# GLA levels by growing queries and keys in place, and projection sections in another order

## The chip, the cores and the metric

One core of a Trainium2 chip runs one program. The metric is the device time of one execution in microseconds, as the median of several. The engines are TensorE (PE; its weight loads are listed as PEld), VectorE (DVE), ScalarE (ACT), GpSimd (POOL) and SyncE (SP), each with its own queue that runs in order, beside 16 DMA engines.

## The reference

One decoder layer over 512 tokens of width 1024, in float32: a token mixer of gated linear attention (GLA, 4 heads of key width 128 and value width 256) beside latent attention (8 heads), gated and projected, then a squared-ReLU MLP of width 4096, each with a residual and a layer norm. The part that the change touches is GLA:

```python
q_g, k_g, v_g, r_g, a_lr, q_lat, kv_lat, gate_logits = jnp.split(h @ w_in, offsets, axis=-1)
log_a = jax.nn.log_sigmoid(a_lr @ w_gla_a2 + b_gla_a2) / 16
# S_t = diag(a_t) S_{t-1} + k_t^T v_t,  o_t = q_t S_t
...
y_gla = (rms_norm(o_gla) * jax.nn.silu(r_g)) @ w_o_gla
```

In other words o_i is the sum over j <= i of (q_i . k_j, channel by channel times the product of the decays a over j+1..i) times v_j.

## The kernel before

Everything is kept transposed or by token tiles of 128. A float32 product is made of three matmuls on parts that are rounded to a shorter format: high by high, high by low, low by high. So each weight tile is loaded by SP (`wraw`), its high half is made by ACT (`whi`, line 180) and its low half by DVE (`wlo`, line 181). `pump` keeps the loads two and the splits one group ahead, in the order in which `plan` was called.

**Projection sections.** After the latents, queries and keys, the columns of `w_in` are multiplied in sections of 512 columns: 8 steps of 12 large matmuls each, into four PSUM banks. `proj_v(hp)` makes the values of heads 2hp and 2hp+1 and empties each bank by ACT (`vh`, line 106) and DVE (`vl`, line 107). `proj_r(hp)` makes the output gate: `th` is a tanh on ACT (line 600), `rg` a product on DVE that reads the bank (line 603). The gate sections `g` need one tanh on ACT for each bank (`gt`, line 958), and `mla_qr` makes the rotary queries. A section can start on a bank only when the one before has emptied it. The order is v0, r0, v1, r1, g0, g1, qr0, g2, g3, qr1 (g0 and g1 are the halves of the first branch's gate, g2 and g3 of the second's).

**Lanes.** Beside the sections run two generators, stepped once in each of a section's 8 steps: `lane_levels`, which makes the score matrices of the four heads in turn (`gla_levels`), and `lane_out`, which makes a head's output (`gla_out`) as soon as its scores, values and output gate are there. The order of the instructions in the queues is set by a scheduler when the program is built.

**Levels.** For each block size s = 1, 2, 4, ... 256 a level makes the scores between the right half of a block of 2s tokens (queries) and its left half (keys). `rp` holds two planes of 512 sums of log decays, for the keys from a token to the end of its block, for the queries from the start of the block. A level takes E = exp(rp/16) on ACT (line 651), multiplies by the queries and keys on DVE into M (line 658, two halves of 256 tokens; line 654 above 64), and doubles the reach of the sums on DVE (`advance`, line 634). PE multiplies M by itself (line 692; 695 at 128; transposes at 256, line 699), and DVE copies the result under a mask into `SD` (line 667). `products` makes the diagonal: `pr` on POOL (line 614), `qkp` high on ACT (616) and low on POOL (617), for the next head at s = 16.

Of the kernel before, what the change touches and what calls it, by code (L numbers as in the profile page):

```python
# [10 lines left out]
F32 = mybir.dt.float32  # L11
# [4 lines left out]
AF = mybir.ActivationFunctionType  # L16
# [3 lines left out]
P = 128  # L20
# [32 lines left out]
def tile_hybrid_block(ctx: ExitStack, tc: tile.TileContext, I, out, dbg=None):  # L53
# [50 lines left out]
    def split(src, hi, lo, scale=None):  # L104
        if scale is None:
            act(hi, src, AF.Copy)
# [31 lines left out]
    def plan(name, c0, n, k_lo=0, k_hi=None, heads=None, res=False, per=2):  # L138
        w = I[name]
        K = w.shape[0] // P  # L140
        k_hi = K if k_hi is None else k_hi
        idx = []
        for k0 in range(k_lo, k_hi, per):
            nk = min(per, k_hi - k0)
            if heads is None:
                src = w.rearrange("(k p) n -> p k n", p=P)
                dmas = [(slice(0, nk), src[:, k0:k0 + nk, c0:c0 + n], None)]
            else:
                hw, h0, nh = heads
# [135 lines left out]
        PL["lat", i] = plan("w_in", C_A + i * half, half, res=True)  # L285
    PL["q"] = plan("w_in", C_Q, T)
    PL["k"] = plan("w_in", C_K, T)
    for hp in range(2):
        PL["v", hp] = plan("w_in", C_V + hp * T, T)
        PL["r", hp] = plan("w_in", C_R + hp * T, T)  # L290
    def plan_qr(g):
        PL["qr", g] = plan("w_q_b", NOPE, 4 * ROPE, heads=(HQ, 4 * g, 4), per=4)

    for br in range(2):
        for mb in range(2):
            PL["g", br, mb] = plan("w_in", C_G + br * D + mb * T, T)
        plan_qr(br)

    def plan_pair(pr):
        PL["qn", pr] = plan("w_q_b", 0, 2 * P, heads=(HQ, 2 * pr, 2))  # L300
# [308 lines left out]

    QKP = [None] * GH  # L610

    def products(h, qk):
        pr = B([P, T], F32, "pr")
        gtt(pr, qk[:, 0, :], qk[:, 1, :], op=ALU.mult)
        QKP[h] = [B([P, T], F32R, "qkp") for _ in range(2)]
        act(QKP[h][0], pr, AF.Copy)
        gtt(QKP[h][1], pr, f(QKP[h][0]), op=ALU.subtract)

    def gla_levels(h):
        qk = QK[h]  # L620
        QK[h] = None
        rp = A([P, 2, T], F32, "rp")
        nc.vector.tensor_copy(rp[:, 1, :], GL[h])
        nc.gpsimd.memset(rp[:, 0, :], 0.0)
        SD = B([P, NT, P], F32, "SD")
        s128 = kq = None

        def advance(s):
            v = rp[:, 0, :]

            def view(off, side, step):
                return bass.AP(tensor=v.tensor, offset=v.offset + off, ap=[v.ap[0], [side, 2], [2 * s, T // (2 * s)], [step, s]])
            new = view(0, T + s, 1)
            vtt(new, new, view(T + 2 * s - 1, -s, 0), op=ALU.add)  # L634

        def half_lr(t2, s, i):
            v = t2[:, 0, :]
            return bass.AP(tensor=v.tensor, offset=v.offset + 2 * i * P,
                           ap=[v.ap[0], [2 * s, P // s], [T + s, 2], [1, s]])

        def packed(M, s, i):
            v = M[:, i, 0, :]
            return bass.AP(tensor=v.tensor, offset=v.offset,
                           ap=[v.ap[0], [2 * s, P // s], [s + (-2 * P if i else 2 * P), 2], [1, s]])

        def taken(v, s, step):
            return bass.AP(tensor=v.tensor, offset=v.offset + s, ap=[v.ap[0], [step, 2], [2 * s, P // s], [1, s]])

        def vec(s):
            E = B([P, T], F32, "E")  # L650
            act(pairs(E, s), lr(rp, s), AF.Exp, scale=1.0 / 16.0)  # L651
            if s > 64:
                M = B([P, T], F32, "M")
                vtt(pairs(M, s), pairs(E, s), lr(qk, s), op=ALU.mult)
            else:
                M = B([P, 2, 2, P], F32, "M")
                for i in range(2):
                    vtt(packed(M, s, i), pairs(E[:, 2 * i * P:2 * (i + 1) * P], s), half_lr(qk, s, i), op=ALU.mult)  # L658
            if s < 256:
                advance(s)  # L660
            return M

        def take(s, p):
            nonlocal s128, kq
            if s <= 64:
                mk = lmask[:, LEVELS.index(s)].rearrange("p o u (n s) -> p o (u n) s", s=s)
                nc.vector.copy_predicated(taken(SD[:, 0, :], s, 2 * P - s), mk, taken(p[:, :2 * P], s, -s))
            elif s == 128:
                s128 = B([P, 2, 2, P], F32R, "s128")
                split(p[:, :256].rearrange("p (a b) -> p a b", b=P), s128[:, 0], s128[:, 1])  # L670
            else:
                split(p[:, :256], kq[:, 0, 0], kq[:, 0, 1])


        if h == 0:
            products(0, qk)
        s = 1
        M = vec(1)
        yield
        diag = PX()  # L680
        for w in range(2):
            mm(diag, ones, QKP[h][w], start=w == 0, stop=w == 1)
        prev = None
        while s < T:
            if s == 2:
                vtt(SD, diag.rearrange("p (t i) -> p t i", i=P), ident[:, None, :].to_broadcast([P, NT, P]), op=ALU.mult)
            if s == 16 and h + 1 < GH:
                products(h + 1, QK[h + 1])
            p = PX()
            if s <= 64:  # L690
                for u in range(2):
                    mm(p[:, u * P:(u + 1) * P], M[:, 0, u, :], M[:, 1, u, :], start=True, stop=True)  # L692
            elif s == 128:
                for i in range(2):
                    mm(p[:, i * P:(i + 1) * P], M[:, 2 * i * P:(2 * i + 1) * P],
                       M[:, (2 * i + 1) * P:(2 * i + 2) * P], start=True, stop=True)
            else:
                for j in range(2):
                    nc.tensor.transpose(p[:, j * P:(j + 1) * P], M[:, j * P:(j + 1) * P], ident)
                kq = A([P, 2, 2, 256], F32R, "kq")  # L700
                split(M[:, 256:], kq[:, 1, 0], kq[:, 1, 1])
            if prev is not None:
                take(*prev)
            prev = (s, p)
            s *= 2
            if s < T:
                M = vec(s)
            yield
        sd = A([P, 2, NT, P], F32R, "sd")
        p = PX()  # L710
        for u in range(2):
            nc.tensor.transpose(p[:, u * P:(u + 1) * P], SD[:, 2 + u, :], ident)
        act(sd[:, 0, :2], SD[:, :2], AF.Copy)
        gtt(sd[:, 1, :2], SD[:, :2], f(sd[:, 0, :2]), op=ALU.subtract)
        take(*prev)
        yield
        pt = p[:, :2 * P].rearrange("p (u i) -> p u i", i=P)
        split(pt, sd[:, 0, 2:], sd[:, 1, 2:])
        SS[h] = (sd, s128, kq)
        if h != 2:  # L720
            yield
# [218 lines left out]
            step(t_lv)  # L940

    WID[0] = 3
    proj_v(0)
    proj_r(0)
    finish(t_lat2)
    proj_v(1)
    proj_r(1)
    t_gla = [t_lv, t_out]


    gt = [None] * NK
    for br in range(2):
        for mb in range(2):
            def ev_g(a, ps):
                m = mb * 4 + a
                if gt[m] is None:
                    gt[m] = A([P, 2, T], F32, "gt")
                act(gt[m][:, br, :], ps, AF.Tanh, scale=0.5, bias=hbg[:, br * NK + m:br * NK + m + 1])
            gemm_fm(PL["g", br, mb], hT, T, ev_g)
        mla_qr(br)  # L960
    hT = None


# [361 lines left out]
```

## Time and profile before

| | us |
|---|---|
| median of 3 runs | 888.38 |
| the three runs | 887.48, 892.6, 888.38 |
| the profiled execution, whole | 887.85 |
| its span, first to last instruction | 885.9 |
| PE busy, matmuls | 863.7 |
| DVE busy | 584.4 |
| ACT busy | 438.9 |
| POOL busy | 134.1 |

The profile is of one execution, 887.85 us long by the device's own count; the span that its tables cover is 2 us shorter. Matmuls overlap, so a matmul's duration is longer than its distance to the next one: the distance tells the rate. A row of a group shows the line, engine, operation, tiles (out<-in) and count, then busy us, mean ns of one, and the idle time of the engine just before them with who ended it. In a timeline a row is start, duration, engine, line, operation, and in brackets the idle time before it. The levels run from about 98 to 260 us of the span.

### The profile page before, as it was taken

Reading aid. Unit: us, or ns where it says so; the run is one execution under the profiler, and the core shown is the slowest. Engines: PE = TensorE matmul, PEld = TensorE weight load, DVE = VectorE, ACT = ScalarE, POOL = GpSimd, SP = SyncE. Lnnn points to the kernel's source line nnn. Section 1 sums busy time; section 2 is a strip of 40 time slices with the busy share of each in tenths; the row PEclk is TensorE's granted clock in tenths of the full one; section 3 lists DMA queues with packets and bytes.
Section 4 is the critical chain, followed back from the end, with each engine's and each line's share of the span. In section 5 each row is a group of like instructions: output and inputs, shape, how many; then the busy total and the mean of one; then the engine's idle time right before and its main releaser. Section 6 shows DMA issues by size and latency. Waiting matters only on the chain.

```text
span 885.9 us, 11470 instructions
## 1 busy us (share of the span) xinstructions
PE 863.7 (97%) x4336; PEld 735.9 (83%) x4336; DVE 584.4 (66%) x989; ACT 438.9 (50%) x737; POOL 134.1 (15%) x159
## 2 busy tenths in 40 slices
PE   5999999999999999999999999999999999999995
PEld 5988888887888888888888888988888888888884
DVE  7834894867665234557866797886557646754687
ACT  5546553634444334435654414565457546735661
POOL 2203320111002010000000013004400520242022
PEclk9999999999999999999999999999999999999998
DMA  7413223221323223111307628006941990398075
GB/s 235 145 48 95 72 72 95 72 72 48 90 72 88 74 84 101 54 43 54 116 25 264 190 71 285 1 0 164 293 114 29 260 253 28 71 305 195 1 189 96
DMA packets 63415, 101.13 MB, mean 114 GB/s; under 512 B 7777, under 2 KB 31764, under 8 KB 63360
## 3 DMA queue, kind: packets, MB, share of 16 engines
q1 hardware_dynamic: 48400, 64.04, 23.5%
q0 software_dynamic: 13040, 32.71, 15.5%
q10 hardware_dynamic: 1920, 3.66, 1.2%
q8 instruction: 34, 0.56, 0.3%
q14 instruction: 21, 0.17, 0.1%
HBM read 82.56 MB, written 3.67 MB: 97 GB/s over the span
## 4 chain that ended last, share of the span: by engine, by line
PE 95%; DVE 2%; ACT 1%; DMA 1%; issue 0%; POOL 0%; POOLq 0%; SPq 0%; DVEq 0%; ACTq 0%
PE mm L231 16%; PE mm L232 16%; PE mm L233 16%; PE mm L266 6%; PE mm L264 6%; PE mm L265 6%; PE px L1170 3%; PE px L1172 3%; PE px L1171 3%; PE mm L1170 2%; PE mm L1172 2%; PE mm L1171 2%; PE px L692 1%; PE px L868 1%; PE px L266 1%; PE px L265 1%
## 5 line engine op out<-in xcount | busy, mean ns | idle before, releaser
L181 DVE TENSOR_TENSOR wlo<-wraw,whi 128x1024 fp32r<-128x1024 f32 (+2 forms) x102 | 117.5, 1152 | 137.1 <-ACT whi L180 130.9
L231 PE MATMUL mm<-h,whi 128*128 128x512 f32 x416 | 163.3, 393 | 1.1 <-DVE rg L603 1.1
L232 PE MATMUL mm<-h,whi 128*128 128x512 f32 x416 | 163.0, 392 | 0.0
L233 PE MATMUL mm<-h,wlo 128*128 128x512 f32 x416 | 156.1, 392 | 0.0
L180 ACT ACTIVATE whi<-wraw 128x1024 fp32r<-128x1024 f32 (+2 forms) x102 | 99.9, 979 | 109.6 <-PE mm L232 66.3
L231 PEld LDWEIGHTS mm<-h,whi 128*128 128x128 f32 x416 | 78.6, 189 | 16.9 <-DVE rg L603 1.3
L232 PEld LDWEIGHTS mm<-h,whi 128*128 128x128 f32 x416 | 78.6, 189 | 16.0
L233 PEld LDWEIGHTS mm<-h,wlo 128*128 128x128 f32 x416 | 78.4, 189 | 16.1
L1198 POOL DMA_DIRECT2D res<-ev x54 | 47.5, 985 | 238.0 <-ACT ev L1196 190.7
L265 PE MATMUL mm<-wlo,h 128*128 128x512 f32 x128 | 50.5, 395 | 0.0
L266 PE MATMUL mm<-whi,h 128*128 128x512 f32 x128 | 50.3, 395 | 0.0
L264 PE MATMUL mm<-whi,h 128*128 128x512 f32 x128 | 49.2, 398 | 0.0
L1252 ACT ACTIVATE relu<-mm 128x512 f32<-128x512 f32 x32 | 18.8, 596 | 57.0 <-PE mm L233 57.0
L651 ACT ACTIVATE E<-rp 128x512 f32<-128x512 f32 x36 | 23.9, 665 | 28.3 <-DVE rp L634 27.4
L658 DVE TENSOR_TENSOR M<-E,qk 128x256 f32<-128x256 f32 x56 | 26.7, 501 | 15.4 <-ACT E L651 15.3
L355 POOL TENSOR_TENSOR mv<-mv,mhalf 128x1 f32<-128x1 f32 x4 | 4.1, 1036 | 208.9 <-DVE mv L354 208.9
L180 ACT ACTIVATE xh<-wraw 128x1024 fp32r<-128x1024 f32 (+1 forms) x20 | 19.0, 959 | 26.2 <-PE mm L266 15.0
L181 DVE TENSOR_TENSOR wlo<-wq,whi 128x1024 fp32r<-128x1024 f32 x15 | 18.4, 1224 | 20.3 <-ACT whi L180 20.3
L266 PEld LDWEIGHTS mm<-whi,h 128*128 128x128 f32 x128 | 24.1, 188 | 4.8
L265 PEld LDWEIGHTS mm<-wlo,h 128*128 128x128 f32 x128 | 24.1, 188 | 4.2
L264 PEld LDWEIGHTS mm<-whi,h 128*128 128x128 f32 x128 | 24.0, 188 | 4.1
L1196 ACT ACTIVATE ev<-mm 128x512 f32<-128x512 f32 x20 | 11.9, 600 | 29.6 <-DMA res<-ev 23.7
(400 smaller groups left out, 2223.6 us busy)
## 6 DMA issues: line engine op xcount, KB each, us to landing
wraw<-in_w_in_dram SPq DMA_DIRECT2D x40, 512.0 KB, 3.7
wraw<-in_w_ff_dram SPq DMA_DIRECT2D x32, 512.0 KB, 8.4
wq<-in_w_ff_dram POOLq DMA_DIRECT2D x32, 512.0 KB, 9.8
res<-ev POOLq DMA_DIRECT2D x54, 256.0 KB, 8.7
wraw<-in_w_o_gla_dram SPq DMA_DIRECT2D x8, 512.0 KB, 3.8
wraw<-in_w_o_mla_dram SPq DMA_DIRECT2D x8, 512.0 KB, 3.4
wraw<-in_w_out_dram SPq DMA_DIRECT2D x8, 512.0 KB, 4.3
wraw<-in_w_in_dram SPq DMA_DIRECT2D x8, 360.0 KB, 4.2
```

The source lines that it names most:

```text
L180: st["ins"] = act(hi[:, :nk, :n], raw[:, :nk, :n], AF.Copy)
L181: vtt(lo[:, :nk, :n], raw[:, :nk, :n], f(hi[:, :nk, :n]), op=ALU.subtract)
L231: mm(o, hi[:, c], xh, start=first, stop=False)
L232: mm(o, hi[:, c], xl, start=False, stop=False)
L233: mm(o, lo[:, c], xh, start=False, stop=last)
L264: mm(o, xh, hi[:, :n], start=opens, stop=False, skip_group_check=share)
L265: mm(o, xh, lo[:, :n], start=False, stop=False, skip_group_check=share)
L266: mm(o, xl, hi[:, :n], start=False, stop=last, skip_group_check=share)
L1170: mm(o, xh[:, c], hi[:, pp, cols], start=opens, stop=False, skip_group_check=True)
L1171: mm(o, xh[:, c], lo[:, pp, cols], start=False, stop=False, skip_group_check=True)
L1172: mm(o, xl[:, c], hi[:, pp, cols], start=False, stop=hf == 1 and pp == 1, skip_group_check=True)
L1198: nc.gpsimd.dma_start(res[tt + t][:, j * T:(j + 1) * T], e, accum_op=ALU.add)
```

## The change

Two things change.

First, the levels. Instead of sums of logarithms that are turned into factors anew in each level, the queries and keys themselves grow. `totals(h)` adds the gate logarithms of each block of 2, 4, ... 128 tokens on POOL (seven adds of 256 down to 4 elements), and takes exp of the gates and of all totals on ACT (two instructions). In `gla_levels` the queries are first multiplied by their own decay (DVE); after each level `grow` multiplies, in place, the right half's queries by the left half's total and the left half's keys by the right half's total (one DVE instruction of 128x512, as `advance` was). A level up to 64 then only packs q and k into M by two copies on ACT (`pack`); at 128 and 256 PE reads q and k themselves. `rp`, E, `advance` and the products M go. `totals(h + 1)` comes with `products(h + 1)` at s = 16.

Second, the order of the sections, in the plan of the weights and in the calls alike: r0, v0, g0, r1, v1, g2, qr0, g1, g3, qr1.

```diff
-    for hp in range(2):
-        PL["v", hp] = plan("w_in", C_V + hp * T, T)
-        PL["r", hp] = plan("w_in", C_R + hp * T, T)
+    ORDER = (("r", 0), ("v", 0), ("g", 0), ("r", 1), ("v", 1), ("g", 2), ("qr", 0), ("g", 1), ("g", 3), ("qr", 1))
...
+    TOT = [None] * GH
+
+    def totals(h):
+        t = TOT[h] = B([P, T], F32, "tot")
+        src, o, n = GL[h], 0, T // 2
+        while n >= 4:
+            a = src.rearrange("p (n two) -> p n two", two=2)
+            src = t[:, o:o + n]
+            gtt(src, a[:, :, 0], a[:, :, 1], op=ALU.add)
+            o += n
+            n //= 2
+        act(GL[h], GL[h], AF.Exp, scale=1.0 / 16.0)
+        act(t[:, :o], t[:, :o], AF.Exp, scale=1.0 / 16.0)
...
-        rp = A([P, 2, T], F32, "rp")
-        nc.vector.tensor_copy(rp[:, 1, :], GL[h])
-        nc.gpsimd.memset(rp[:, 0, :], 0.0)
...
-            new = view(0, T + s, 1)
-            vtt(new, new, view(T + 2 * s - 1, -s, 0), op=ALU.add)
+        def grow(s):
+            new = view(qk[:, 0, :], 0, T + s, 2 * s, 1, s)
+            tot, o = (GL[h], 0) if s == 1 else (TOT[h], T - 2 * T // s)
+            vtt(new, new, view(tot, o + 1, -1, 2, 0, s), op=ALU.mult)
...
-        def vec(s):
-            E = B([P, T], F32, "E")
-            act(pairs(E, s), lr(rp, s), AF.Exp, scale=1.0 / 16.0)
-            if s > 64:
-                M = B([P, T], F32, "M")
-                vtt(pairs(M, s), pairs(E, s), lr(qk, s), op=ALU.mult)
-            else:
-                M = B([P, 2, 2, P], F32, "M")
-                for i in range(2):
-                    vtt(packed(M, s, i), pairs(E[:, 2 * i * P:2 * (i + 1) * P], s), half_lr(qk, s, i), op=ALU.mult)
-            if s < 256:
-                advance(s)
+        def pack(s):
+            M = B([P, 2, 2, P], F32, "M")
+            for i in range(2):
+                act(packed(M, s, i), half_lr(qk, s, i), AF.Copy)
             return M
...
         if h == 0:
+            totals(0)
             products(0, qk)
+        vtt(qk[:, 1, :], qk[:, 1, :], GL[h], op=ALU.mult)
         s = 1
-        M = vec(1)
+        M = pack(1)
...
             if s == 16 and h + 1 < GH:
+                totals(h + 1)
                 products(h + 1, QK[h + 1])
...
-                    mm(p[:, i * P:(i + 1) * P], M[:, 2 * i * P:(2 * i + 1) * P],
-                       M[:, (2 * i + 1) * P:(2 * i + 2) * P], start=True, stop=True)
+                    mm(p[:, i * P:(i + 1) * P], qk[:, 0, 2 * i * P:(2 * i + 1) * P],
+                       qk[:, 1, (2 * i + 1) * P:(2 * i + 2) * P], start=True, stop=True)
...
             prev = (s, p)
+            if s < 256:
+                grow(s)
             s *= 2
-            if s < T:
-                M = vec(s)
+            if s <= 64:
+                M = pack(s)
...
-    proj_v(0)
-    proj_r(0)
-    finish(t_lat2)
-    proj_v(1)
-    proj_r(1)
...
+    for sec, i in ORDER:
+        if sec == "v":
+            proj_v(i)
+        elif sec == "r":
+            proj_r(i)
+            if i == 0:
+                finish(t_lat2)
+        elif sec == "g":
+            gates(i // 2, i % 2)
+        else:
+            mla_qr(i)
```

What it does to the queues is shown where the second output-gate section (r1) ends. PE there, before: the last two banks of r1 (`mm_1745`, `mm_1749`), the matmuls of levels 32 and 64 of the third head (`px_1954`, `px_1999`), and the first bank of g0 (`mm_2008`).

```order
L265 MATMUL mm_1745<-wlo_1870,h_33_171 128x512
L266 MATMUL mm_1745<-whi_1869,h_33_171 128x512
L264 MATMUL mm_1749<-whi_1869,h_33_171 128x512
L265 MATMUL mm_1749<-wlo_1870,h_33_171 128x512
L266 MATMUL mm_1749<-whi_1869,h_33_171 128x512
L692 MATMUL px_1954<-M_1924 128x128 x2
L692 MATMUL px_1999<-M_1960 128x128 x2
L231 MATMUL mm_2008<-h_12_115,whi_1938 128x512
```

PE there, in the changed kernel: the last bank of r1 (`mm_1727`), transposes of the second head's output (`og`), levels 32, 64 and 128 of the third head (`px_1927`, `px_1970`, `px_1991`), and the first bank of v1 (`mm_1975`).

```order
L264 MATMUL mm_1727<-whi_1836,h_33_171 128x512
L786 MATMUL px_1904<-ca,og_1828 128x128 x2
L786 MATMUL px_1904<-ca,og_1829 128x128 x2
L702 MATMUL px_1927<-M_1898 128x128 x2
L265 MATMUL mm_1727<-wlo_1837,h_33_171 128x512
L266 MATMUL mm_1727<-whi_1836,h_33_171 128x512
L702 MATMUL px_1970<-M_1932 128x128 x2
L705 MATMUL px_1991<-qk_750 128x128 x2
L264 MATMUL mm_1975<-whi_1911,h_12_115 128x512
```

Level 128 of that head now stands inside r1, behind level 64 with nothing between, and the section that follows is values, not a gate.

ACT at the same place, before: the last exp of the levels (`E`), the split of a weight tile, the head's output and the tanh of r1's first two banks (`mm_1737`, `mm_1741`).

```order
L651 ACTIVATE E_1889<-rp_1753 128x512
L180 ACTIVATE whi_1938<-wraw_1867 128x1024
L616 ACTIVATE qkp_1914<-pr_1912 128x512
L651 ACTIVATE E_1922<-rp_1753 128x512
L109 ACTIVATE ogT_1928<-px_1895,cb 128x512
L651 ACTIVATE E_1958<-rp_1753 128x512
L109 ACTIVATE ogT_1964<-px_1931,cb 128x512
L600 ACTIVATE th_1979<-mm_1737 128x512
L600 ACTIVATE th_1983<-mm_1741 128x512
```

ACT there, in the changed kernel: `M_1857`, `M_1898` and `M_1932` are the copies of levels 16, 32 and 64, `g_666` and `tot_1877` the next head's gates and totals.

```order
L667 ACTIVATE M_1857<-qk_750 128x8x2x16 x2
L180 ACTIVATE whi_1911<-wraw_1834 128x1024
L627 ACTIVATE g_666<-g_666 128x512
L634 ACTIVATE qkp_1889<-pr_1887 128x512
L109 ACTIVATE ogT_1901<-px_1860,cb 128x512
L667 ACTIVATE M_1898<-qk_750 128x4x2x32 x2
L628 ACTIVATE tot_1877<-tot_1877 128x508
L667 ACTIVATE M_1932<-qk_750 128x2x2x64 x2
L604 ACTIVATE th_1950<-mm_1715 128x512
```

The exp of the next head's totals stands ahead of level 64's copies and of the first tanh of r1.

POOL at the same place, before: the square-root scaling of a head (`grs`), the next head's diagonal, and a memset.

```order
L762 TENSOR_TENSOR grs_1837<-gss_1722,mhalf 128x4
L614 TENSOR_TENSOR pr_1912<-qk_752 128x512
L617 TENSOR_TENSOR qkp_1915<-pr_1912,qkp_1914 128x512
L624 MEMSET rp_2093 128x512
L714 TENSOR_TENSOR sd_2071<-SD_1756,sd_2071 128x256
```

POOL there, in the changed kernel:

```order
L774 TENSOR_TENSOR grs_1806<-gss_1700,mhalf 128x4
L624 TENSOR_TENSOR tot_1877<-g_666 128x256
L632 TENSOR_TENSOR pr_1887<-qk_752 128x512
L624 TENSOR_TENSOR tot_1877<-tot_1877 128x128
L624 TENSOR_TENSOR tot_1877<-tot_1877 128x64
L635 TENSOR_TENSOR qkp_1890<-pr_1887,qkp_1889 128x512
L624 TENSOR_TENSOR tot_1877<-tot_1877 128x32
L624 TENSOR_TENSOR tot_1877<-tot_1877 128x16
L624 TENSOR_TENSOR tot_1877<-tot_1877 128x8
L624 TENSOR_TENSOR tot_1877<-tot_1877 128x4
L726 TENSOR_TENSOR sd_2035<-SD_1731,sd_2035 128x256
```

Four of the seven adds stand behind the low half of `qkp`, which waits for ACT's high half.

More of the change, by code (lines that the diff above doesn't have):

```diff
@@ L287, in tile_hybrid_block @@
     PL["k"] = plan("w_in", C_K, T)
-    for hp in range(2):
-        PL["v", hp] = plan("w_in", C_V + hp * T, T)
-        PL["r", hp] = plan("w_in", C_R + hp * T, T)
+    ORDER = (("r", 0), ("v", 0), ("g", 0), ("r", 1), ("v", 1), ("g", 2), ("qr", 0), ("g", 1), ("g", 3), ("qr", 1))
     def plan_qr(g):
         PL["qr", g] = plan("w_q_b", NOPE, 4 * ROPE, heads=(HQ, 4 * g, 4), per=4)
[L294 to L297, printed above, removed]
+    for sec, i in ORDER:
+        if sec == "v":
+            PL["v", i] = plan("w_in", C_V + i * T, T)
+        elif sec == "r":
+            PL["r", i] = plan("w_in", C_R + i * T, T)
+        elif sec == "g":
+            PL["g", i // 2, i % 2] = plan("w_in", C_G + i * T, T)
+        else:
+            plan_qr(i)
     def plan_pair(pr):
@@ L621, in gla_levels, with view @@
         QK[h] = None
-        rp = A([P, 2, T], F32, "rp")
-        nc.vector.tensor_copy(rp[:, 1, :], GL[h])
-        nc.gpsimd.memset(rp[:, 0, :], 0.0)
         SD = B([P, NT, P], F32, "SD")
         s128 = kq = None
[L628 to L632, printed above, removed]
-            new = view(0, T + s, 1)
-            vtt(new, new, view(T + 2 * s - 1, -s, 0), op=ALU.add)
+        def view(t, off, side, blk, step, s):
+            return bass.AP(tensor=t.tensor, offset=t.offset + off, ap=[t.ap[0], [side, 2], [blk, T // (2 * s)], [step, s]])
+        def grow(s):
+            new = view(qk[:, 0, :], 0, T + s, 2 * s, 1, s)
+            tot, o = (GL[h], 0) if s == 1 else (TOT[h], T - 2 * T // s)
+            vtt(new, new, view(tot, o + 1, -1, 2, 0, s), op=ALU.mult)
         def half_lr(t2, s, i):
@@ L694, in gla_levels @@
                 for i in range(2):
-                    mm(p[:, i * P:(i + 1) * P], M[:, 2 * i * P:(2 * i + 1) * P],
-                       M[:, (2 * i + 1) * P:(2 * i + 2) * P], start=True, stop=True)
+                    mm(p[:, i * P:(i + 1) * P], qk[:, 0, 2 * i * P:(2 * i + 1) * P],
+                       qk[:, 1, (2 * i + 1) * P:(2 * i + 2) * P], start=True, stop=True)
             else:
                 for j in range(2):
-                    nc.tensor.transpose(p[:, j * P:(j + 1) * P], M[:, j * P:(j + 1) * P], ident)
+                    nc.tensor.transpose(p[:, j * P:(j + 1) * P], qk[:, 0, j * P:(j + 1) * P], ident)
                 kq = A([P, 2, 2, 256], F32R, "kq")
-                split(M[:, 256:], kq[:, 1, 0], kq[:, 1, 1])
+                split(qk[:, 1, 256:], kq[:, 1, 0], kq[:, 1, 1])
             if prev is not None:
@@ L942, in tile_hybrid_block, with gates, ev_g @@
     WID[0] = 3
-    proj_v(0)
-    proj_r(0)
-    finish(t_lat2)
-    proj_v(1)
-    proj_r(1)
     t_gla = [t_lv, t_out]
     gt = [None] * NK
[L952 to L960, printed above, removed]
+    def gates(br, mb):
+        def ev_g(a, ps):
+            m = mb * 4 + a
+            if gt[m] is None:
+                gt[m] = A([P, 2, T], F32, "gt")
+            act(gt[m][:, br, :], ps, AF.Tanh, scale=0.5, bias=hbg[:, br * NK + m:br * NK + m + 1])
+        gemm_fm(PL["g", br, mb], hT, T, ev_g)
+    for sec, i in ORDER:
+        if sec == "v":
+            proj_v(i)
+        elif sec == "r":
+            proj_r(i)
+            if i == 0:
+                finish(t_lat2)
+        elif sec == "g":
+            gates(i // 2, i % 2)
+        else:
+            mla_qr(i)
     hT = None
```

## The prediction

> **What bounds the kernel now.** I first read the busy times and the table by stage, then who PE waits for, and then row by row the one place where PE waits.
>
> ```profile
> PE 863.7 (97%) x4336; PEld 735.9 (83%) x4336; DVE 584.4 (66%) x989; ACT 438.9 (50%) x737; POOL 134.1 (15%) x159
> ...
> 180.00:200.00 20.00, 20.00 (x105) 17.10 (x104) 14.03 (x27) 8.45 (x16) 4.16 (x3) 1.00 0.23 72
> 200.00:220.00 20.00, 18.37 (x89) 15.19 (x88) 14.77 (x26) 9.11 (x17) 1.86 (x3) 0.91 0.18 53
> 220.00:240.00 20.00, 20.00 (x107) 17.24 (x106) 11.96 (x22) 9.79 (x22) 1.23 (x1) 1.00 0.31 87
> ...
> 600.00:620.00 20.00, 20.00 (x90) 16.58 (x89) 12.77 (x12) 11.29 (x16) 9.58 (x12) 1.00 0.70 178
> ```
>
> The columns after the stretch are its length and the busy time of PE, PEld, DVE, ACT and POOL, then granted clock, DMA share and GB/s. PE is busy 97%. A busy PE isn't yet a full one, so I check the rate: in an undisturbed stage 90 matmuls take 20 us, 0.222 us each. The stretches of the GLA stage beside 200:220 hold 105 and 107 (small ones among them) with no idle time. Only 200:220 falls short, with 18.37 us busy and the clock at 0.91.
>
> ```profile
> PE mm L231 <- DVE rg L603: 1.1, 1, 1.1
> PE px L692 <- DVE M L658: 0.5, 1, 0.5
> PE mm L264 <- ACT gt L958: 0.3, 1, 0.3
> ```
>
> These are all of PE's waits between 100 and 300 us: who waited, for whom, total, times, longest. The first two are one event, where the second output-gate projection ends and the first gate section starts:
>
> ```profile
> 204.22 0.60 PE L692 MATMUL px<-M 128*128 128x128 f32 x4
> ...
> 204.47 0.75 DVE L658 TENSOR_TENSOR M<-E,qk 128x256 f32<-128x256 f32 x2
> ...
> 205.37 0.68 PE L692 MATMUL px<-M 128*128 128x128 f32 x4 [0.55 <-DVE M L658]
> ...
> 206.40 1.87 DVE L603 SCALAR_TENSOR_TENSOR rg<-th,mm 128x512 f32<-128x512 f32 x3
> 207.13 0.50 PE L231 MATMUL mm<-h,whi 128*128 128x512 f32 x1 [1.08 <-DVE rg L603]
> ...
> 208.17 0.60 PE L232 MATMUL mm<-h,whi 128*128 128x512 f32 x1
> 208.57 0.63 PE L233 MATMUL mm<-h,wlo 128*128 128x512 f32 x1
> ...
> 211.55 0.42 PE L232 MATMUL mm<-h,whi 128*128 128x512 f32 x1
> ```
>
> PE waits 0.55 us for the packed operand of level 64, then 1.08 us until DVE has emptied the first PSUM bank. DVE is late because it forms M and the sums as well. Then matmuls start 0.40 us apart (208.17 to 208.57). From 208.17 to 211.55 eight take 3.38 us where eight at 0.222 us take 1.78:
>
> ```profile
> 206.00:208.00 2.00, 0.92 (x5) 0.74 (x5) 2.00 (x4) 1.73 (x3) 0.00 (x0) 1.00 0.00 0
> 208.00:210.00 2.00, 2.00 (x7) 1.58 (x6) 2.00 (x4) 0.00 (x0) 0.00 (x0) 0.55 0.00 0
> ```
>
> The granted clock is 0.55 just behind the wait. So the event costs 0.55 + 1.08 + 1.60 = 3.2 us. With the 0.3 us for `gt`, 3.5 us is all that a faster supply of the levels can win: 0.4% of the time.
>
> **The change part by part.** The prices:
>
> ```profile
> L658 DVE TENSOR_TENSOR M<-E,qk 128x256 f32<-128x256 f32 x56 | 26.7, 501 | 15.4 <-ACT E L651 15.3
> L634 DVE TENSOR_TENSOR rp<-rp 128x512 f32<-128x512 f32 x32 | 23.1, 722 | 0.0
> L654 DVE TENSOR_TENSOR M<-E,qk 128x512 f32<-128x512 f32 x8 | 5.5, 685 | 0.7 <-ACT E L651 0.7
> L651 ACT ACTIVATE E<-rp 128x512 f32<-128x512 f32 x36 | 23.9, 665 | 28.3 <-DVE rp L634 27.4 <-DVE rp L623 0.9
> L106 ACT ACTIVATE kq<-M 128x256 fp32r<-128x256 f32 x4 | 1.7, 420 | 1.9 <-DVE M L654 1.9
> L600 ACT ACTIVATE th<-mm 128x512 f32<-128x512 f32 x8 | 4.5, 597 | 2.5 <-PE mm L266 2.3
> L958 ACT ACTIVATE gt<-mm,hbg 128x512 f32<-128x512 f32 x16 | 10.8, 691 | 8.8 <-PE mm L233 5.1 <-issue 2.8 <-PE px L754 1.0
> L603 DVE SCALAR_TENSOR_TENSOR rg<-th,mm 128x512 f32<-128x512 f32 x8 | 5.3, 682 | 1.7 <-ACT th L600 1.7
> L616 ACT ACTIVATE qkp<-pr 128x512 fp32r<-128x512 f32 x4 | 2.5, 620 | 0.0
> L180 ACT ACTIVATE whi<-wraw 128x1024 fp32r<-128x1024 f32 x84 | 88.9, 1059 | 83.5 <-PE mm L232 46.2 <-PE mm L266 13.7 <-issue 7.8
> L757 ACT ACTIVATE osq<-px 128x256 f32<-128x256 f32 x16 | 6.1, 384 | 18.7 <-PE px L755 18.7
> L767 DVE SCALAR_TENSOR_TENSOR og<-px,grs,rg 128x256 f32<-128x256 f32 x16 | 6.6, 473 | 0.0
> L617 POOL TENSOR_TENSOR qkp<-pr,qkp 128x512 fp32r<-128x512 f32 x4 | 8.2, 2038 | 39.4 <-ACT qkp L616 39.4
> L453 POOL TENSOR_TENSOR kr<-kt,kt 128x64 f32<-128x64 f32 x4 | 2.6, 680 | 3.0 <-DVE kt L452 3.0
> L991 POOL COPY cmask<-cb 128x128 f32<-128x128 f32 x1 | 0.5, 517 | 3.6 <-DVE SD L667 3.6
> L762 POOL TENSOR_TENSOR grs<-gss,mhalf 128x4 f32<-128x4 f32 x4 | 4.4, 1096 | 45.3 <-DVE gss L760 45.3
> ...
> 133.95 0.89 PE px L692 x8
> ```
>
> Behind the bar stand busy us and mean ns; the last row is from the chain of waits, eight small PE records in 0.89 us, so 0.11 each.
>
> DVE loses the M products and the sums, 26.7 + 5.5 + 23.1 = 55.3 us (four copies of the gates not counted). It gains 32 products of 0.722 us, of the shape of the sums, and four whole-row products of about 0.69 (the 128x512 row of L654), 25.9 us: some 29 us less, off the path but for the event above.
>
> ACT loses 36 E, 23.9 us. It gains 56 copies of half a tile. No strided copy is in the trace; the contiguous one took 0.420 us, so 23.5 us. E with its strided reads took 0.665 where a contiguous 128x512 took 0.620, so up to 8% more is possible. Eight Exp of 0.62 us come on top: about 5 us more in all, beside PE. The table loads stay as many.
>
> POOL loses four memsets and gains 28 adds of 256 down to 4 elements. The small ones are the unknown price, p. A 128x64 add took 0.68 with DVE at work beside it, a 128x128 copy 0.517, and 128x4 with a power 1.10. I take 0.5, near the copy; the ends are 0.1 (256 elements' price cut by length) and 1.1.
>
> PE's work is the same in number and shape; level 128 and the transposes of 256 read q and k themselves, and so wait for DVE's last product instead of for M. The sections move with all their weight loads, in the same count and order of halves, so SP's queue only fetches other columns.
>
> Now the path. The chain per level was Exp, two products: 0.665 + 1.00. It becomes product, two copies: 0.722 + 0.84. No shorter, but DVE is no longer the engine that also empties banks, makes wlo and grows the sums. The tightest place is again where the second output gate ends, now followed by the values. I count from the end of level 16's copies. ACT there has in line: whi 1.06, the next head's Exp 0.62, qkp 0.62, ogT 0.7 (near whi's half and qkp), two copies of level 32, 0.84: 3.8 us. Then comes the second Exp of the next head's totals, which waits for POOL: POOL takes the low half of qkp (2.04) once ACT is through with its qkp at 2.3, so until 4.3, and then four small adds, 4p. With p = 0.5: Exp 6.3 to 6.9, copies of level 64 to 7.8, product to 8.5, first bank emptied by rg at 9.2.
>
> PE from the same zero: it comes to level 16's matmul about 3.6 us later. That is worked out: from the third row block of the heads' output to that matmul PE has 62 large matmuls (13.8) and 30 records of 0.11 (3.3), 17.1; ACT and DVE need in that time five levels (7.8), two whi (2.1), three squares (1.2, and 0.5 for their read-outs) and four output scalings (1.9), 13.5 in series. The power of 1.1 between them and what overlaps I let cancel; 17.1 - 13.5 = 3.6. From there eight large matmuls (1.8), a set of transposes (0.44) and four level products (0.44 each, four records) bring it to 3.6 + 4.0 = 7.6, where it wants the first bank: 1.6 us of wait, in pieces (level 64, level 128, bank). With p = 0.1 it is none; with p = 1.1 it is 4.0.
>
> Whether 1.6 us in pieces halves the clock again I leave open: 1.63 did, 0.3 did not. I charge half of 1.60. At the other boundaries PE has more slack: where values end and the gates begin, the heads' output matmuls come first and the one level due there has had 44 large matmuls' time; where a gate section ends, one ACT pass of 0.69 us a bank (`gt`) meets PE's 0.67 a bank with transposes and output matmuls between. There I charge nothing; if that cover goes, each costs about a us. The 0.3 us at `gt` should go, since the output matmuls now stand ahead of the rotary queries.
>
> The sum, against the profiled execution's 887.85 us (0.5 below the median of 888.38): 887.85 - 3.2 - 0.3 + 1.6 + 0.8 = 886.75, say 886.7.
>
> [...]
>
> **The rivals.**
>
> *The totals hold ACT up (slower).* The small adds cost 1.1 us like the 128x4 row, and ACT's second Exp, ahead of level 64's copies and of all `th`, waits for them. At the end of the second output gate the wait is 4.0 us and the clock falls for sure: 4.0 + 1.6 - 3.5 = +2.1, 890.0. At the end of the first output gate the same Exp stands ahead of whi and `th`, with some 1 us to spare before PE wants the bank: another 1 to 2.7, so 891 to 892.7. It decides from p of about 0.75 (2.6 us of wait with a fallen clock cost more than 3.5). For: 1.10 is a row of the trace for so few elements. Against: those rows take a power, and 0.68 and 0.517 don't.
>
> *POOL's adds hold DVE.*
>
> ```profile
> 191.83 1.60 POOL L614 TENSOR_TENSOR pr<-qk 128x512 f32<-128x512 f32 x1
> ...
> 192.18 1.53 DVE L658 TENSOR_TENSOR M<-E,qk 128x256 f32<-128x256 f32 x1
> ```
>
> One product that takes 0.50 us by its mean took 1.53 beside a POOL product. If the adds in that chain hold DVE for their length, its products of levels 32 and 64 come up to 4p = 2 us later: 888.7. [...]
>
> *Nothing gained.* The level chain isn't shorter (1.56 against 1.67 us), the event moves to the new boundary with the same 1.6 us and the fallen clock: 887.6.
>
> *It is worse at every boundary.* If ACT, not DVE, is the late engine in all four heads (strided copies at 0.6 instead of 0.42 make a level 2 us), each head loses 2 + 1.6 us: 4 x 3.6 - 3.5 = +10.9, 898.8.
>
> **How the numbers follow.** Chances: forecast 0.42 (between 884.3, all 3.5 won, and 887.5), totals hold ACT 0.20, adds hold DVE 0.15, nothing gained 0.14, every boundary 0.07, left over 0.02. The range leaves out the last two and the far end of the first rival: from 0.8 below the forecast's lower bound (nearly the 0.9 by which two of the runs before, 887.48 and 888.38, differ) to inside the first rival's span, 883.5 to 892.0. One per cent is 8.9 us, about what a measurement here can tell from no change. A gain of that size has no place when 3.5 us are there to be won: 0.01. Slower by over 1% is the last rival: 0.08. Within: 0.91.
>
> **What would show it.** Right: no wait of PE for `rg` or M over 1 us, DVE's busy time down by some 29 us and ACT's up by 5, the small adds at 0.4 to 0.6 us, at most one clock drop near 200 us. Wrong: adds near 1.1 with ACT idle ahead of the second Exp; strided copies above 0.5; PE waits at two or more boundaries, each with a granted clock near 0.55 behind it.

## The result and the profile after

The changed kernel takes 883.3 us (median of six runs, 882.6 to 883.7), the kernel before 888.3 in the runs beside it (886.8 to 892.6): a ratio of 0.9938, 95% interval 0.9917 to 0.9959. That is 5.0 us less, where 1.7 had been forecast, and 0.2 below the range. The profiled execution took 883.6 us, against 887.85 before. The executions of the kernel before spread from 886.3 to 894.7 us in the series below, those of each variant by less than 2 us, but for the one with the longest wait (three executions of 1400 us and more are left out throughout).

The busy line of the page, PE's waits over the whole span, and the window in which PE waited before:

```profile
PE 861.2 (98%) x4336; PEld 734.4 (83%) x4336; DVE 562.8 (64%) x925; ACT 442.6 (50%) x765; POOL 139.7 (16%) x183
```

```profile
PE px L374 <- DMA wraw<-in_w_in_dram: 9.1, 1, 9.1
PE mm L266 <- POOL h L382: 1.2, 1, 1.2
PE mm L231 <- ACT h L377: 0.3, 1, 0.3
PE mm L265 <- DVE xl L181: 0.2, 1, 0.2
```

```profile
200.00:220.00 20.00, 20.00 (x108) 17.06 (x107) 16.66 (x29) 13.38 (x29) 3.21 (x6) 1.00 0.22 58
```

The four waits lie at the start of the program and around layer norms. Those for `rg`, M and `gt` are gone, nothing has come in their place, and the window from 200 to 220 us has 20.00 us of PE at a clock of 1.00 where it had 18.37 at 0.91.

A yardstick for the stretch that the change touches: from PE's first diagonal matmul (`qkp`, first head) to its first matmul on the heads' output (`ogT`). It holds the same 1144 records in both kernels. The tile view gives the first and last start; first of before, then of the changed kernel:

```profile
L682 PE MATMUL px<-qkp,ones x4: 389/391/477, 100.7 to 127.4; 128*128 128x512 f32 x4
L231 PE MATMUL mm<-ogT,whi x12: 389/389/397, 321.8 to 329.3; 128*128 128x512 f32 x12
```

```profile
L691 PE MATMUL px<-qkp,ones x4: 389/390/476, 101.6 to 128.2; 128*128 128x512 f32 x4
L231 PE MATMUL mm<-ogT,whi x16: 389/389/475, 317.7 to 329.2; 128*128 128x512 f32 x16
```

321.8 - 100.7 = 221.1 against 317.7 - 101.6 = 216.1: 5.0 us, the whole difference of the medians. From there to the start of PE's last matmul both kernels take 554.1 us. (The two profiled executions differ by less, 4.25 us, since the changed one came 0.8 us later to this stretch, and was as late already at its first section on the queries.)

The prices that were open, by groups of lines (busy us, mean ns, idle before):

```profile
L667 ACT ACTIVATE M<-qk 128x256 f32<-128x256 f32 x56 | 24.0, 456 | 16.9 <-DVE qk L649 16.7
L649 DVE TENSOR_TENSOR qk<-qk,tot 128x512 f32<-128x512 f32 x28 | 20.1, 719 | 19.9 <-ACT M L667 19.7 <-PE px L705 0.2
L685 DVE TENSOR_TENSOR qk<-qk,g 128x512 f32<-128x512 f32 x4 | 4.6, 1153 | 0.0
L635 POOL TENSOR_TENSOR qkp<-pr,qkp 128x512 fp32r<-128x512 f32 x4 | 6.4, 1600 | 41.4 <-ACT qkp L634 41.4
L624 POOL TENSOR_TENSOR tot<-tot 128x32 f32<-128x32 f32 x4 | 1.9, 462 | 0.2
L624 POOL TENSOR_TENSOR tot<-tot 128x16 f32<-128x16 f32 x4 | 1.3, 326 | 0.2
L624 POOL TENSOR_TENSOR tot<-tot 128x8 f32<-128x8 f32 x4 | 1.1, 282 | 0.2
L624 POOL TENSOR_TENSOR tot<-tot 128x4 f32<-128x4 f32 x4 | 0.8, 200 | 0.3
```

The four small adds take 0.32 us each on average (0.462, 0.326, 0.282, 0.200), a strided copy 0.456. And the place on which the forecast rested, the end of the second output gate, in the timeline:

```profile
196.92 0.72 ACT L667 ACTIVATE M<-qk 128x256 f32<-128x256 f32 x2 [2.53 <-DVE qk L649]
...
199.71 1.51 POOL L635 TENSOR_TENSOR qkp<-pr,qkp 128x512 fp32r<-128x512 f32 x1 [2.19 <-ACT qkp L634]
...
201.18 1.54 POOL L624 TENSOR_TENSOR tot<-tot 128x32 f32<-128x32 f32 x4
...
202.29 0.60 PE L702 MATMUL px<-M 128*128 128x128 f32 x4
...
202.75 0.63 ACT L628 ACTIVATE tot<-tot 128x508 f32<-128x508 f32 x1 [1.72 <-POOL tot L624]
...
204.76 1.27 DVE L607 SCALAR_TENSOR_TENSOR rg<-th,mm 128x512 f32<-128x512 f32 x2
...
205.90 0.61 PE L705 MATMUL px<-qk 128*128 128x128 f32 x4
...
206.26 0.47 PE L264 MATMUL mm<-whi,h 128*128 128x512 f32 x1
```

Zero is the end of level 16's copies, 196.92 + 0.72 = 197.64. ACT does wait for POOL's small adds, 1.72 us. But the first bank is emptied at half of `rg`'s two, 204.76 + 0.64 = 205.40, so at +7.8, and PE comes for it at 206.26, +8.6. There are 0.86 us to spare where the forecast had 1.6 us missing.

### The profile page after: what moved, and what is told of

The parts are those of the page before. It is cut to its first block, busy times and chain, and to the rows that moved or that the text cites. A ratio compares the mean times of both kernels' runs of the same rounds, so it can differ in the third digit from the quotient of the medians.

```text
span 881.8 us, 11466 instructions
## 1 busy us (share of the span) xinstructions
PE 861.2 (98%) x4336; PEld 734.4 (83%) x4336; DVE 562.8 (64%) x925; ACT 442.6 (50%) x765; POOL 139.7 (16%) x183
## 4 chain that ended last, share of the span: by engine, by line
PE 96%; DMA 2%; DVE 1%; issue 0%; ACT 0%; POOLq 0%; DVEq 0%; SPq 0%; POOL 0%; ACTq 0%
PE mm L231 16%; PE mm L232 16%; PE mm L233 16%; PE mm L266 6%; PE mm L265 6%; PE mm L264 6%; PE px L1186 3%; PE px L1187 3%; PE px L1188 3%; PE mm L1187 2%; PE mm L1188 2%; PE mm L1186 2%; PE px L702 1%; PE px L880 1%; PE px L264 1%; PE px L266 1%
## 5 line engine op out<-in xcount | busy, mean ns | idle before, releaser
L649 DVE TENSOR_TENSOR qk<-qk,tot 128x512 f32<-128x512 f32 x28 | 20.1, 719 | 19.9 <-ACT M L667 19.7
L667 ACT ACTIVATE M<-qk 128x256 f32<-128x256 f32 x56 | 24.0, 456 | 16.9 <-DVE qk L649 16.7
```

## The experiments

The theory after this reading: the kernel before loses its time at one event (DVE late at the end of the second output gate, and a slower clock behind it), and the change takes the whole of it away with nothing given back. Open were which of its two parts does it and by what, how near the new order is to a wait, and why the event was worth more than the sum of its parts in the forecast. In each table row or sentence "stretch" is the yardstick above.

### One part alone

The new levels with the old order of sections:

```diff
-    ORDER = (("r", 0), ("v", 0), ("g", 0), ("r", 1), ("v", 1), ("g", 2), ("qr", 0), ("g", 1), ("g", 3), ("qr", 1))
+    ORDER = (("v", 0), ("r", 0), ("v", 1), ("r", 1), ("g", 0), ("g", 1), ("qr", 0), ("g", 2), ("g", 3), ("qr", 1))
```

> The new levels with the sections in the order of before (both value and output gate projections ahead of the gates). Theory A (the levels alone win: DVE no longer forms M and grows the sums): PE's waits for rg and M and the clock drop behind the second output gate go, 883 to 884.5. Theory B (the order of the sections wins, by putting a gate section between the two head pairs): the waits stay, in other names (rg, or the products), with a granted clock near 0.5 behind them: 886.5 to 888.5. Theory C (both are needed): between, 885 to 887, a wait left at that boundary but without a clock drop.

884.84 us (884.5 to 885.8), ratio 0.9948 (0.9925 to 0.997), stretch 217.7. PE's waits in the stretch, all of them:

```profile
PE mm L231 <- DVE rg L607: 0.3, 1, 0.3
PE px L766 <- DVE gst L107: 0.2, 1, 0.2
```

The clock stays at 1.00. The levels alone win most of it. The time lies between the ranges of theory A (up to 884.5) and theory C (from 885), and a wait without a clock drop is left, which is theory C's sign.

The old levels with the new order (the loop over `ORDER` in the kernel before):

```diff
-    for hp in range(2):
-        PL["v", hp] = plan("w_in", C_V + hp * T, T)
-        PL["r", hp] = plan("w_in", C_R + hp * T, T)
+    ORDER = (("r", 0), ("v", 0), ("g", 0), ("r", 1), ("v", 1), ("g", 2), ("qr", 0), ("g", 1), ("g", 3), ("qr", 1))
...
```

> The levels of before (Exp of running sums, two products) with the sections in the new order. Theory A (levels win): some boundary still has PE waiting for DVE (rg, M or the split of the values) by 1 us or more, 887 to 889. Theory B (order wins): no wait of PE above 0.3 us between 100 and 320 us, 883.5 to 885. Theory C (both needed): a smaller wait, 885 to 887.

885.51 us (884.2 to 886.1), ratio 0.9951 (0.9931 to 0.9972), stretch 218.4. PE's waits in the stretch:

```profile
PE mm L264 <- DVE rg L607: 0.8, 1, 0.8
PE mm L264 <- ACT gt L955: 0.4, 1, 0.4
```

Theory B is wrong that the order removes the waits, A that it does nothing. Each part alone takes most of the loss away, 3.4 and 2.7 us of stretch out of 5.0 with the clock drop among it, since each makes PE wait less for the same bank. The two gains don't add up: what is won in common can be won once. Both are needed for no wait at all, which was theory C.

### By what the levels win

The prediction gave DVE's load as the reason. So the copies were put back on DVE, in the kernel with the old order, where the event is:

```diff
-                act(packed(M, s, i), half_lr(qk, s, i), AF.Copy)
+                nc.vector.tensor_copy(packed(M, s, i), half_lr(qk, s, i))
```

> The new levels with the old order of sections, and the packed copies M made on DVE instead of ACT. If the new levels win because DVE has less to do (theory A as written: M and the growing sums off DVE), the 56 copies, some 0.35 to 0.5 us each, put the load back: PE's wait for rg at the end of the second output gate comes back to about 1 us and the time rises from 884.8 to 886 or 887. If they win because a level is a shorter chain (no Exp between two DVE steps), a copy on the same engine as the product shortens it further: 884.3 to 884.9, with no wait for rg above 0.4 us.

884.70 us (884.0 to 885.3), stretch 217.8 against 217.7 with the copies on ACT. The busy line of its page, the row of the copies and PE's waits in the stretch:

```profile
PE 861.7 (98%) x4336; PEld 734.1 (83%) x4336; DVE 577.7 (65%) x981; ACT 422.4 (48%) x709; POOL 146.0 (17%) x183
```

```profile
L667 DVE COPY M<-qk 128x256 f32<-128x256 f32 x56 | 19.4, 371 | 0.5
```

```profile
PE px L702 <- DVE M L667: 0.4, 1, 0.4
PE px L766 <- DVE gst L107: 0.2, 1, 0.2
```

DVE now does per level two copies and a product, 2 x 0.37 + 0.72 = 1.46 us, close to the kernel before (two products and a sum, 2 x 0.50 + 0.72 = 1.72), and nothing is lost, nor gained: the wait for `rg` is gone, one of 0.4 for M has come. DVE's load by itself was not the main reason. The expectation's other reason, that a level is a shorter chain without E on ACT, isn't shown either, though the time lies in the range that went with it. The rows around the bank, first of the kernel before, then of this one (PE comes to level 32 at 204.22 and 204.16 us):

```profile
203.11 0.63 ACT L651 ACTIVATE E<-rp 128x512 f32<-128x512 f32 x1 [1.20 <-DVE rp L634]
203.81 0.75 DVE L110 SCALAR_TENSOR_TENSOR ogT<-px,cb,ogT 128x512 fp32r<-128x512 f32 x1
...
205.14 0.69 DVE L634 TENSOR_TENSOR rp<-rp 128x512 f32<-128x512 f32 x1
205.74 0.74 DVE L110 SCALAR_TENSOR_TENSOR ogT<-px,cb,ogT 128x512 fp32r<-128x512 f32 x1
```

```profile
204.50 0.48 DVE L667 COPY M<-qk 128x256 f32<-128x256 f32 x2
204.90 0.67 DVE L607 SCALAR_TENSOR_TENSOR rg<-th,mm 128x512 f32<-128x512 f32 x1
205.50 0.68 DVE L649 TENSOR_TENSOR qk<-qk,tot 128x512 f32<-128x512 f32 x1
```

In the kernel before E is ready at 203.74, but M of level 64 starts only at 204.47, behind a part of a head's output (`ogT`) on DVE: DVE's line holds M up there, not E. Behind M stand the sum and a second `ogT`, and `rg` starts at 206.40. With the copies on DVE the operand of level 64 comes hardly sooner (204.98 against 205.22), but `rg` stands right behind it, ahead of the next product, and starts at 204.90. So the long wait went with DVE's line, which the scheduler laid out anew. No run changes the levels with that line held: how much of the gain is the levels' own and how much the new line is open.

### How near the next wait is

The rival that had most weight was that the totals' exp holds ACT up. First the four small adds of each head were done twice and three times, the same values again:

```diff
-            gtt(src, a[:, :, 0], a[:, :, 1], op=ALU.add)
+            for _ in range(3 if n <= 32 else 1):
+                gtt(src, a[:, :, 0], a[:, :, 1], op=ALU.add)
```

> The changed kernel with the four small adds of each head's totals (32 down to 4 elements) done twice; the second time gives the same values. ACT's second Exp comes about 1.5 us later. If ACT's line behind that Exp is what sets the time at the end of the second output gate and PE has 0.9 us to spare there, PE waits 0.6 us for rg or level 64, and the time rises by 0.5 to 0.7 us; with a clock drop behind it by 2.2. If the totals lie off the path, nothing moves (within 0.3 us).

> The changed kernel with the four small adds done three times. ACT's second Exp comes about 3.1 us later. If PE has 0.9 us to spare, PE waits 2.2 us and the granted clock falls to half for 3 us behind it as it did in the kernel before: 2.2 + 1.6 = 3.8 us more, 887.4. If a clock drop takes a longer wait than that: 2.2 more, 885.8. If the totals lie off the path, nothing moves.

883.58 and 883.48 us, stretch 216.1 in both, no wait of PE. That looks like "off the path", but the test missed its aim. ACT's timeline with three times the adds:

```profile
202.82 0.73 ACT L668 ACTIVATE M<-qk 128x256 f32<-128x256 f32 x2 [2.36 <-DVE qk L650]
203.45 1.55 ACT L604 ACTIVATE th<-mm 128x512 f32<-128x512 f32 x3
...
205.45 0.65 ACT L629 ACTIVATE tot<-tot 128x508 f32<-128x508 f32 x1
```

The exp of the totals (L629) now stands behind level 64's copies and three tanh, where it stood ahead of them: the scheduler saw longer adds when the program was built and laid ACT's line out anew. So ACT's line was tied down as it is in the changed kernel, and only the fourth head's adds repeated:

```diff
-        act(t[:, :o], t[:, :o], AF.Exp, scale=1.0 / 16.0)
+        HOLD["exp"] = act(t[:, :o], t[:, :o], AF.Exp, scale=1.0 / 16.0)
...
-            for i in range(2):
-                act(packed(M, s, i), half_lr(qk, s, i), AF.Copy)
+            with tc.issue_after(HOLD["exp"].ins) if (h, s) == (2, 64) else nullcontext():
+                for i in range(2):
+                    cp = act(packed(M, s, i), half_lr(qk, s, i), AF.Copy)
+            if (h, s) == (2, 64):
+                HOLD["copy"] = cp
...
-            act(th, ps, AF.Tanh, scale=0.5)
+            with tc.issue_after(HOLD["copy"].ins) if hp else nullcontext():
+                act(th, ps, AF.Tanh, scale=0.5)
```

> The changed kernel with ACT's line held as it is in the changed kernel at the end of the second output gate (the fourth head's second Exp, then level 64's copies, then the tanh), and the four small adds of that head done twice, 1.5 us more. In the run with the adds doubled and nothing held, the Exp had slipped behind the tanh; here it can't. If PE has 0.9 us to spare there, PE waits about 0.6 us: 883.3 to 884.0 without a clock drop, 885 to 886 with one. If the line doesn't matter: as the changed kernel.

> The same with the adds three times, 3.1 us more. If PE has 0.9 us to spare, it waits about 2.2 us: 885.5 without a clock drop, 887 to 888 with one behind the wait as in the kernel before (granted clock near 0.55, some 1.6 us lost). If the line doesn't matter: as the changed kernel, within 0.3 us.

> The changed kernel with ACT's line held and the fourth head's four small adds done four times, 4.6 us more than the changed kernel. With the adds three times PE waited 1.11 us in one piece and the time rose by 1.8 us, with no clock drop. If each further repeat adds its own length (1.5 us), PE waits about 2.6 us: 886.6 to 887.0 without a clock drop. If a single wait of that length also makes the clock fall as 0.55 + 1.08 us did in the kernel before, 888.2 to 888.7, with a granted clock near 0.5 behind it. The recorded order moves PE's matmuls of level 64 further back than with three, which can hide up to 1 us of it: 885.6 at the least.

| small adds | us (median) | stretch | wait of PE listed | lowest clock in 2 us |
|---|---|---|---|---|
| once (the changed kernel) | 883.3 | 216.1 | none | 1.00 |
| twice | 884.31 | 217.1 | 0.2 | 1.00 |
| three times | 884.91 | 218.0 | 1.1 | 1.00 |
| four times | 887.28 | 220.3 | 2.3 | 0.51 |

PE's place in the last of them, in the timeline, and the two windows behind the wait:

```profile
208.04 1.22 PE L709 MATMUL px<-M 128*128 128x128 f32 x4 [2.27 <-ACT M L672]
```

```profile
208.00:210.00 2.00, 1.96 (x9) 1.96 (x10) 2.00 (x5) 1.93 (x4) 0.00 (x0) 0.51 0.38 37
210.00:212.00 2.00, 2.00 (x7) 1.60 (x7) 2.00 (x4) 1.82 (x5) 0.00 (x0) 0.64 0.60 229
```

The rival's mechanism is real: with the order held, longer adds do hold ACT up and PE behind it. With the adds twice, ACT's exp comes 1.5 us later against the rows around it and the stretch grows by 1.0; with three times 2.7 and 1.8. So 0.5 to 0.9 us are hidden, which agrees with the 0.86 us read from the trace. It doesn't decide here, because the adds cost 0.39 us at this place (0.32 on average) and not the 0.75 or more from which it would. Its price was too high as well: with the adds three times, 4.23 us of POOL's time or 1.06 for each of four, the stretch grew by 1.8 us at a clock of 1.00, where the rival had 4.0 us of wait and a fallen clock. The 0.86 us are those of the bank. PE's wait in that run is for level 64's copies, which stand ahead of the bank and in the changed kernel have 1.3 us to spare (they end at 204.12, PE comes at 205.45). No run holds the order with the adds done once. With twice and three times the medians rise by 1.0 and 1.6, against 0.6 and 2.2 expected without a clock drop. With four times the profiled execution took 888.03 with the drop, against 888.2 to 888.7 expected; of all twelve, three took 885.5 to 886.1 and nine 887.1 to 888.5, so one profile doesn't speak for all.

### Why the event was worth more than the forecast said

The kernel before was profiled four more times.

> The kernel before, once more with a profile. Its executions on this chip spread from 886.3 to 894.2 us, with a mean granted clock of 0.997 to 0.992, while the changed kernel stays within 1.1 us at 0.997. If the spread comes from the wait at the end of the second output gate, the stretch from 200 to 220 us holds it: a clock of 1.00 there in an execution near 886, below 0.91 (a longer drop) in one near 893, and nothing else differs. If another place of the kernel drops its clock in the long executions, another stretch shows a clock below 1.

> As the run ahead of it: the kernel before, a second profile, to catch an execution of the other kind.

> The kernel before, a third profile. The second showed the same waits (1.1 and 0.6 us) with the clock at 1.00 behind them and 1.5 us less time than the first. If the clock drop is a matter of chance behind the same waits, this profile has the waits again (1.0 to 1.2 and 0.5 to 0.6) and either no drop (887 to 887.5) or one of 3 us or so (888 to 889); executions near 893 would show a longer drop there or a second one elsewhere.

> As the run ahead of it, a fourth profile of the kernel before.

888.78, 887.27, 893.53 and 887.15 us. The waits are there each time. The second one's, and its windows over the event, which are to be held against those with a clock of 0.55 in the prediction:

```profile
PE mm L231 <- DVE rg L603: 1.1, 1, 1.1
PE px L692 <- DVE M L658: 0.6, 1, 0.6
PE mm L264 <- ACT gt L958: 0.3, 1, 0.3
```

```profile
206.00:208.00 2.00, 0.76 (x5) 0.60 (x5) 2.00 (x5) 2.00 (x5) 0.00 (x0) 1.00 0.00 0
208.00:210.00 2.00, 2.00 (x9) 1.63 (x10) 2.00 (x4) 0.51 (x1) 0.00 (x0) 1.00 0.00 0
```

Behind the same waits the clock fell in three of the five profiles and stayed at 1.00 in two. The stretch is 219.8 in both without a drop and 221.1 to 221.4 in the three with one. So the waits alone are worth 219.8 - 216.1 = 3.7 us, and the drop another 1.3 to 1.6.

What decides whether it falls isn't shown. PE's waits at the event and the clock granted over it, in the lowest of the stretches read (in brackets):

| profile | PE's waits, us | clock |
|---|---|---|
| the kernel before, first | 0.55, then 1.08 | 0.55 (208 to 210) |
| before_a | 0.5, then 1.1 | 0.50 (210 to 212) |
| before_b | 0.6, then 1.1 | 1.00 (each 2 us from 204 to 214) |
| before_c | 0.5, then 1.1 | 0.91 (200 to 220) |
| before_d | 0.5, then 1.1 | 1.00 (200 to 220) |
| adds held, three times | 1.1 | 1.00 (each 2 us from 204 to 214) |
| adds held, four times | 2.3 | 0.51 (208 to 210) |

The two profiles without a drop have waits as long as the three with one. In the first profile the clock is at 0.50 from 208.2 to 211.6 us, so for 3.4 us.

The execution of 893.53 us has the event with its drop and a second one, far behind the change. Its waits there, and the row of ACT that PE waits behind:

```profile
PE px L370 <- ACT lnt L375: 3.2, 1, 3.2
```

```profile
543.46 1.06 ACT L180 ACTIVATE whi<-wraw 128x1024 fp32r<-128x1024 f32 x1 [5.92 <-DMA wraw<-in_w_ff_dram]
```

```profile
540.00:560.00 20.00, 16.76 (x106) 14.77 (x105) 15.26 (x29) 8.18 (x14) 3.36 (x5) 0.91 0.60 217
```

ACT waits 5.92 us for a weight tile of the MLP, PE 3.2 us for ACT, and the clock falls there too, to 0.91 over these 20 us. From the end of the stretch to PE's last matmul this execution takes 559.1 us, 5.0 more than the others. This part of the program is not touched by the change, and in two of the kernel's other profiles ACT waited 1.27 us (the first) and 2.53 us (before_b) for the same tile and PE not at all. Of the kernel before, 20 of 71 timed executions over all series took more than 891 us, of the changed kernel and the variants beside it none of 85. That is too uneven for chance, so the change and each of its parts seem to have a hand in it; by what is open, and only one of the long executions has a profile.

## Why the prediction was wrong

**Where the time goes before.** Right: one place, the waits for M and `rg` with the clock behind them. In no run of the changed kernel or of a part of it does the profile list a wait of more than 0.4 us at another boundary of the levels.

**The ceiling, "3.5 us is all that a faster supply of the levels can win".** Too low. It added up the waits that the profile lists, 0.55 + 1.08 + 0.3 = 1.93 us, and the clock. The distance from start to start tells more. In the kernel before, the second matmul behind the event starts here:

```profile
207.47 0.39 PE L232 MATMUL mm<-h,whi 128*128 128x512 f32 x1
```

Eight level products at 0.11 and one large matmul take 1.1 us; from 204.22, in the prediction's row of the first four, to 207.47 they took 3.25. That is 2.1 us lost where 1.63 were listed. And at `gt`:

```profile
264.09 0.38 PE L753 MATMUL px<-gst,kq 128*128 128x256 f32 x1
264.46 0.39 PE L753 MATMUL px<-vh,sd 128*128 128x256 f32 x1
...
265.53 0.28 PE L755 MATMUL px<-gst,kq 128*128 128x256 f32 x1
266.10 0.39 PE L264 MATMUL mm<-whi,latT 128*128 128x256 f32 x1 [0.29 <-ACT gt L958]
```

Matmuls of this size start 0.12 us apart (264.80 and 264.92 in the same profile); here two distances are 0.37 and 0.57, so 0.7 us are lost where 0.3 was listed. Together 2.8 us, against 3.7 by the yardstick without a clock drop; with 1.57 us for the drop (3.38 less eight at 0.226, the distance from 203.54 to 204.22 being three) 4.4, against 5.0. Some 0.6 to 0.9 us isn't placed. The term for the clock, 1.60, was right for the profiled execution, but it is one of two outcomes.

**The new wait, "1.6 us of wait" and "half of 1.60" for the clock.** This is the step that failed most: 2.4 us that didn't come. Both sides of it were off. ACT's line was shorter: the low half of `qkp` took 1.51 us and not 2.04, the four adds 1.54 and not 2.0 (p was 0.385 there, within its bounds), so the exp began at +5.1, not 6.3, and the bank was empty at +7.8, not 9.2. PE was later: it came to level 16 at 202.29, +4.65, where the working of 17.1 - 13.5 had given 3.6, and to the bank at +8.6, not 7.6. Each error is about 1 us; in a difference of two sums of 13 to 17 us that is what decides. The size of the gain hung on it, and the forecast's value stood on it, with the case without the wait only as the end of its span. Between the forecast, 886.75, and the 883.3 measured lie 3.45 us: the 2.4 us of this term and the 1.5 by which the ceiling was too low, less 0.45, since the forecast starts from the profiled 887.85 and the median is 888.3. The time below the range goes back to the ceiling: with no wait at all the prediction's own sum is 884.3.

**DVE's relief as the reason.** Only in part, as the run with the copies on DVE showed. "No shorter" for the level's chain was right by durations (0.72 + 2 x 0.456 = 1.63 us against 1.67 before). What the account left out is the order on DVE's line: with the copies on DVE and DVE about as loaded as before (577.7 us against 584.4), `rg` started 1.5 us earlier. How much of the gain goes back to that is open. The instructions were priced well: copies 0.456 for 0.42 with up to 8% more, products 0.719 for 0.722, ACT +3.7 us for "about 5". DVE's busy time fell by 21.6 us, not 29: on the page neighbours that overlap count once, in the groups that were added up they don't (its instructions' own durations fell by 31.0 us).

**The rivals.** The totals' exp: the mechanism is there, 1.72 us of idle ACT, and covered. POOL's adds holding DVE: no product with the levels' totals was slowed at this place (0.68 to 0.77 us, five of L649), but one of L685 was beside the low half of `qkp` (1.47 us, where the mean is 1.153), off the path. "Nothing gained" and "worse at every boundary" fall with the empty list of waits.

## What to carry to other kernels

Price a stall by the starts of the instructions around it, against the same instructions elsewhere, and not by the waits that the profile lists: here at least 2.8 us against 1.9. Where a forecast hangs on which of two long lines comes last, the difference of the two sums is known no better than their errors, so the case without the wait belongs into the range as an equal. And a scheduler that knows a price moves work out of its way: to test a cost, hold the order, or the experiment measures the scheduler.

## What the runs showed of the hardware

Behind PE's waits of 0.5 to 0.6 and 1.1 us at one place the granted clock fell in three of five profiles of one program and stayed at 1.00 in two; in the first it was at 0.50 for 3.4 us. Behind a single wait of 1.1 us it stayed at 1.00, in one profile. A single wait of 2.3 us cost 4.2 us of stretch in a profile with a drop. Small GpSimd adds cost 0.20 to 0.46 us for 4 to 32 elements a partition: eight times the elements, 2.3 times the price; those of 64 took 0.294. The four smallest took 1.54 us at the event and 1.27 on average. A strided DVE copy of 128x256 took 0.371 us where ACT took 0.456.
